# Score products of a stick-breaking attention: the second pass over 128 rows instead of 64

## Chip, cores and metric

One core of a Trainium2 chip runs the whole program. The metric is the device time of one execution in microseconds, as the median of the runs. Engine names: TensorE (PE; its weight loads are listed apart as PEld), VectorE (DVE), ScalarE (ACT), GpSimd (POOL) and SyncE (SP, which issues most DMAs).

## What is computed

One step of a two-layer hybrid network in float32, for 1024 prompt tokens and 8 sequences with 8 sample tokens each, width 1024. Layer 0 mixes by stick-breaking attention (16 heads of 64), layer 1 by an RWKV-7 recurrence; each is followed by a feed-forward block. The part that matters here is the prompt's attention of layer 0:

```python
z = (jnp.einsum('bqhd,bkhd->bhqk', q, k).astype(jnp.float32) * (SB_HEAD_DIM ** -0.5)
     + bias.astype(jnp.float32)[None, :, None, None])
mask = k_pos[None, :] < q_pos[:, None]
log_beta = jax.nn.log_sigmoid(z)
log_1mb = jnp.where(mask, log_beta - z, 0.0)
tail = lax.cumsum(log_1mb, axis=3, reverse=True) - log_1mb
a = jnp.where(mask, jnp.exp(log_beta + tail), 0.0)
return jnp.einsum('bhqk,bkhd->bqhd', a.astype(v.dtype), v)
```

So a weight is beta of its key times the product of 1 - beta over the later keys before the query.

## The kernel before

The tokens are worked on in two parts: the first has 576 prompt tokens, the second the other 448 and the 64 sample tokens. Features lie on the partitions, 128 to a feature tile; a feature tile holds two heads of 64.

Every dense layer (`dense`, L354 to L368) multiplies in three passes of rounded parts: a float32 value is split into an upper part (rounded to the fp32r format, "hi") and the lower rest ("lo"), and hi by hi, hi by lo and lo by hi are added up in one bank of PSUM (L364 to L366). After each such triple `step` is called; it advances a generator of background work by a number of yields. The prompt's attention is such background work: `background` (L1588) runs `attention(0)` at two yields a step and `attention(1)` at three, behind the projection of the second part and the output and feed-forward layers of the first. After `attention(1)` has done the prompt's queries, it goes on with the samples and the paged cache, in buffers that take the place of those of the prompt. The program is built with a framework that orders each engine's instructions by a simulated timeline (L1798) and puts in the semaphores; each engine then works through its own list in order.

For each of the eight feature tiles `att_stacks` (L526) loads q, k and v and prepares, for each of the two heads, with a the head's own 64 partitions and b the other 64:

- qh: the rounded upper part of q, on both halves (L546 on VectorE for a, L547 on ScalarE for b);
- kk: the upper part of k on a (L548) and its lower part on b (L549), both on VectorE;
- ql: the lower part of q on a (L550, GpSimd). One tile ql of 128 partitions serves both heads, half each.

q, k, qh, kk and ql have one buffer each, so the next feature tile's parts are written when the last products that read them are done.

`att_prompt` (L574) then goes over query tiles, the one of 64 queries first (both heads in one tile, q and k unsplit, L602), then those of 128 queries of one head. The keys are taken in pieces of up to 512. A score tile of one head is two passes into one bank of PSUM:

1. L604: qh by kk over 128 rows, which adds up hi(q) by hi(k) and hi(q) by lo(k);
2. L606: ql[a] by kk[a] over 64 rows, which adds lo(q) by hi(k).

`stick` (L555) follows: a sigmoid on ScalarE (L561) gives beta, the mask is laid on by GpSimd (L612 or L614), GpSimd makes 1 - beta (L564), with one column more at the end (L566 or L568), VectorE runs a multiplying scan from the last key to the first (L570) and multiplies beta by it (L571). TensorE transposes the weights (L127, called from L624), ScalarE copies them out of PSUM (L628), and TensorE multiplies them by v (L637). The output of a feature tile is copied to ot and written to DRAM (L642).

Of the kernel before, what the change touches and what calls it, by code (L numbers as in the profile page):

```python
# [10 lines left out]
F32 = mybir.dt.float32  # L11
# [9 lines left out]
NT = 8            # feature tiles of 128  # L21
TP = 1024         # prompt tokens
TS = 64           # sample tokens, column 1024 + 8 * sequence + step
T = TP + TS
PAGES = 16
ROWS = 2
# [19 lines left out]
class Part:  # L46
    """Columns o to o + W of the tokens, the first NP of them of the prompt; chunks of 64 tokens
    of the prompt from c0 on; ch: what fits into a bank of PSUM."""
# [45 lines left out]
class Kern:  # L94
# [19 lines left out]
    def copy(self, out, in_, eng=None):  # L114
        """PSUM or SBUF to SBUF, on ScalarE and VectorE in turn."""
        if eng is None:
            eng = "a" if self.flip() else "v"
        if eng == "a":
            self.nc.scalar.copy(out, in_)  # L119
        elif eng == "v":  # L120
            self.nc.vector.tensor_copy(out, in_)  # L121
        else:
            self.nc.gpsimd.tensor_copy(out, in_)
# [23 lines left out]
    def load_params(self, groups, tmp, ps, tag):  # L147
        """Vectors of features: rows of 128 on partitions, then features on partitions."""
# [46 lines left out]
    def behind(self, work, rate=1.0):  # L195
        """Work that goes on behind dense layers: rate steps of it behind every step of those."""
        self.work, self.rate, self.owed = work, rate, 0.0
# [11 lines left out]
    def beside(self, work, rate):  # L209
        """Other work beside dense layers, rate steps of it behind every step of those."""  # L210
        for _ in self.side:
            pass
        self.side, self.side_rate, self.side_owed = work, rate, 0.0

    def until(self, done):
        """The work behind, until done() (or its end)."""
        while not done():
            if next(self.work, self) is self:
                break
# [5 lines left out]
    def ada_steps(self, s, ps, tag, blocks=range(12)):  # L225
        """mod[:, j, v]: feature tile j of shift (0-7), scale (8-15), gate (16-23); vector v.
        The scale tiles end up as norm gain * (1 + scale)."""
# [44 lines left out]
    def rms(self, x, pt, tmp, ps, tag, slot, rslot=None):  # L272
        """1 / sqrt(mean square + eps) of every token, on all partitions: [128, W]."""
# [26 lines left out]
    def modulate(self, s, f, x, R, pt, t):  # L300
        """t = x * R * A of feature tile f, of samples with B added; returns B of the prompt."""
# [18 lines left out]
    def norm_split(self, s, x, R, pt, pool, tmp, slot):  # L320
        """Rounded parts of (x * R) * A + B."""
# [32 lines left out]
    def dense(self, w, mts, hi, lo, pt, ps, evac):  # L354
        """w: DRAM [K, M]; evac(m, c0, n, psum)."""
# [14 lines left out]
    def residual(self, s, x, pt, tmp):  # L370
        """evac of a dense layer: x += gate * out."""
# [17 lines left out]
    def load_x(self, pt, pool, ps, early):  # L389
        """Generator; the tiles are in self.x. early: all loads first."""  # L390
# [27 lines left out]
    def to_tokens(self, m, pt, t, dst_p, dst_s, tmp, ps):  # L418
        """Feature tile m of the columns of pt; rows of tokens to DRAM."""
# [43 lines left out]
    def load_split(self, src, pt, pool, tmp, parts):  # L463
        """Generator: rounded parts of feature tiles in DRAM."""
# [9 lines left out]
    def ahead(self, flag, src, pt, pool, tmp, xpool=None):  # L474
        """Generator: what the layer after a mixer needs, once the mixer is through: rounded parts
        of its output, and the tokens, to self.next."""
# [7 lines left out]
    def ffn(self, s, x, hi, lo, pt, pool, tmp, ps):  # L484
        """x += gate * (relu(h @ w_up) ** 2) @ w_down, the hidden layer 512 at a time."""
# [22 lines left out]
    def att_setup(self, lp):  # L508
# [7 lines left out]
        # of the two heads of a feature tile, 64 rows each  # L516
# [9 lines left out]
    def att_stacks(self, m, pt, sp):  # L526
        """Rounded parts of q and k of the two heads of tile m, the parts of k on top of each other."""
# [13 lines left out]
        ql = sp.tile([128, SLOT], F32R, tag="ql", name="ql")[:, :pt.NP]  # L541
        for hd in range(2):
# [6 lines left out]
            nc.vector.tensor_sub(kk[b], k[a], kk[a].bitcast(F32))  # L549
            nc.gpsimd.tensor_sub(ql[a], q[a], qh[a].bitcast(F32))  # L550
            qs.append(qh)
            ks.append(kk)
        return q, k, qs, ql, ks, v

    def stick(self, z, w, bias, bp, tag, carry, mask):  # L555
        """z: scores in PSUM [128, w], keys in order; returns weights a and the product of 1 - beta."""
# [17 lines left out]
    def att_prompt(self, m, pt, sp, bp, ps):  # L574
        """Generator over the query tiles (128 of a head, or 64 of both) of the two heads of tile m."""
        nc = self.nc
        q, k, qs, ql, ks, v = self.att_stacks(m, pt, sp)
# [7 lines left out]
        for c, end in sorted(tiles, key=lambda t: t[1] - t[0]):  # L585
# [7 lines left out]
            for j, (e0, e1) in enumerate(pieces):  # L593
# [3 lines left out]
                for x, hs in enumerate(heads):  # L597
                    z = ps.tile([128, 512], F32, tag="z", name="z")
                    for hd in hs:
                        a = self.R2[hd]  # L600
                        if both:
                            nc.tensor.matmul(z[a, :w], q[a, qc], k[a, e0:e1], start=True, stop=True)  # L602
                            continue
                        nc.tensor.matmul(z[:, :w], qs[hd][:, qc], ks[hd][:, e0:e1], start=True,  # L604
                                         stop=False)
                        nc.tensor.matmul(z[:, :w], ql[a, qc], ks[hd][a, e0:e1], start=False,  # L606
                                         stop=True)
# [44 lines left out]
    def page_k(self, sp, r):  # L652
        """[128 (feature / 256, key % 32), key / 32, feature % 256]"""
# [17 lines left out]
    def att_sample(self, sp, bp, ps):  # L671
        """Generator over the pieces (new keys, then two pages at a time, last pages first) of the
        sequences. Features are in 8 tiles of 128 rows (feature / 256, feature % 32), so that a
        page's blocks of 32 rows and columns, transposed by VectorE, are its transpose; tiles 2g and
        2g + 1 hold heads g, 4 + g, 8 + g and 12 + g. Rows of scores: g, head / 4, 8 queries; every g
        has its own columns of the tensor engine."""
# [12 lines left out]
        def queries(b):  # L689
            """Every head's queries in its own columns: [128, tile, 4 heads x 8]."""  # L690
# [56 lines left out]
        for n, (b, j) in enumerate(steps):  # L747
# [27 lines left out]
            if j == 0:  # L775
                # every row's own head, features on partitions
# [15 lines left out]
    def attention(self, i):  # L792
        """Generator: a half of the queries."""
# [72 lines left out]
    def rw_late(self, lp):  # L866
        """What the recurrence needs beyond rw_setup."""
# [11 lines left out]
    def xmix(self, n, f, h, e, pt, c0, w, t):  # L879
        """t = h + (previous token's h - h) * mu[n] of feature tile f, w columns of pt from c0;  # L880
        h starts e columns earlier."""
# [11 lines left out]
    def xsplit(self, n, pt, pool, tmp, parts):  # L893
        """Generator: rounded parts of the mixed input n, to parts."""
# [20 lines left out]
    def rw_norm(self, x, R, pt, pool, tmp):  # L915
        """The normalized input, to DRAM; rounded parts of the mixed input of r."""
# [34 lines left out]
    def rw_shift(self, tmp, ps):  # L951
        """The last token of every sequence."""
# [11 lines left out]
    def lora_mixed(self, ns, f, pt, c0, n, tmp):  # L964
        """Mixed inputs ns of feature tile f, n columns of pt from c0."""
# [10 lines left out]
    def lora_rates(self, pt, tmp, ps):  # L976
        """Generator: the narrow halves of the low-rank products of the rates."""
# [16 lines left out]
    def lora_gate(self, pt, pool, tmp, ps):  # L994
        """Generator: the narrow half of the low-rank product of the gate."""
# [23 lines left out]
    def rw_gate(self, pt, tmp, ps):  # L1019
        """Generator: the wide half of the gate, to DRAM."""  # L1020
# [16 lines left out]
    def dense_to(self, w, hi, lo, pt, tmp, ps, dst, then=None):  # L1037
        """Dense layer to DRAM, one feature tile at a time."""
# [9 lines left out]
    def rw_value(self, m, pt, t, tmp, ps):  # L1048
        """Feature tile m of v, tokens first."""
# [15 lines left out]
    def rw_keys(self, m, pt, k, pp, ps):  # L1065
        """Normalized keys of feature tile m."""
# [11 lines left out]
        # 1 / sqrt: from a guess by the exponent, three Newton steps  # L1078
# [20 lines left out]
    def rw_unit(self, m, i, pp, ps):  # L1099
        """Generator: the chunk products of feature tile m (two heads) that the state isn't needed  # L1100
        for. Rates are 1 + tanh of half the logits, twice the sigmoid."""
# [41 lines left out]
        # key  # L1143
# [9 lines left out]
        # decayed copies  # L1153
# [13 lines left out]
        # stacks: 0, 1 inputs of the solve, 2, 3 outputs, 4, 5 states; of the two heads  # L1167
# [52 lines left out]
    def rw_lanes(self, ms, pt, pool):  # L1220
        """Generator: (I - L)^-1 of diagonal blocks of 32 of the feature tiles ms, a block per
        partition (feature tile, block, head, chunk), by substitution."""
# [33 lines left out]
    def rw_units(self, i):  # L1256
        """Generator: chunk products of a half of the tokens."""
# [21 lines left out]
    def rw_chain(self, m, i, todo, cp, ps):  # L1279
        """Generator over the chunks of feature tile m: the recurrence of the state, and all that  # L1280
        follows up to w_o (put into todo)."""
# [24 lines left out]
        def inverse(n, st, tt, hv, L, x1):  # L1306
            """Inverses of 64 from those of 32."""
# [31 lines left out]
        for gi, (u, n) in enumerate(groups):  # L1339
# [4 lines left out]
            for cc in range(n):  # L1344
# [19 lines left out]
                # the state's rows still hold the chunk's first state  # L1364
# [46 lines left out]
    def rw_samples(self, m, y, cp, ps):  # L1411
        """Generator: the samples' chunk of feature tile m."""
# [11 lines left out]
        # the samples' states, key on partitions  # L1424
# [377 lines left out]
```

## Time and profile before

| what | value |
|---|---|
| median of 3 runs | 4046.95 us (4046.1 to 4064.11) |
| span of the profiled execution | 4045.0 us |
| span to median | 1.95 us |
| mean granted TensorE clock | 0.950 |
| L604, L606: number of each | 160 |
| time in which they run | 256 to 945 us |
| L550: number | 32 |

Profiled times count from the first instruction of the span. In the timeline a matmul's start and duration stand ahead of the engine; durations of matmuls that follow each other overlap, so the distance from start to start, called a step below, is what a matmul costs the engine in a row of them. `64*128 64x512` is a matmul of 64 rows and 128 columns of weights on 512 columns of moving data. A bracket at the end of a row gives the idle time before it and what ended it. In the list of waits the columns are the total in us, the number of times and the longest.

### The profile page before, as it was taken

The page shows a single profiled execution, that of the slowest core. Times are in us where ns is not written, and L with a number is a line of the kernel's source. Part 1 is how long each engine was busy: PE and PEld are TensorE (multiplying, and loading weights), DVE is VectorE, ACT ScalarE, POOL GpSimd, SP SyncE. Part 2 cuts the span into 40 slices and gives each one's busy share as a digit, 9 for nine tenths or more (in the row PEclk, how much of TensorE's full clock was granted, in tenths as well). Part 3 has the DMA queues.
Part 4 walks back from the last instruction along what each step waited for, and adds up shares of the span by engine and source line. Part 5 has one row for each costly group of instructions (what it writes and reads, how often), then busy time and mean ns, then how long its engine had stood idle before and what let it go on. Part 6 is the DMA issues. An engine that isn't in the chain of part 4 may idle for free. (4 is left out here: it accounts for less than half of the span.)

```text
span 4045.0 us, 76587 instructions
## 1 busy us (share of the span) xinstructions
PE 3675.1 (91%) x27756; PEld 2899.0 (72%) x27756; DVE 2499.4 (62%) x4907; ACT 1491.1 (37%) x3132; POOL 1322.8 (33%) x1844
## 2 busy tenths in 40 slices
PE   8989999899887888799779999999889999998998
PEld 6776667677666666577657777665688888876887
DVE  4256777886555455668775555677884666645444
ACT  4123444543121122455333444554434333433332
POOL 1135555563111111222243333433222222233442
PEclk9999999999999999799789999898899999999999
DMA  9965434125999999856645444556735444342332
GB/s 283 292 186 164 153 114 102 49 67 140 236 236 215 216 228 231 239 169 217 180 118 139 127 129 131 173 179 212 215 110 138 116 121 137 96 133 76 102 98 78
DMA packets 873728, 641.63 MB, mean 159 GB/s; under 512 B 174195, under 2 KB 793004, under 8 KB 873350
## 3 DMA queue, kind: packets, MB, share of 16 engines
q1 hardware_dynamic: 804198, 602.12, 52.8%
q10 hardware_dynamic: 69152, 34.61, 3.9%
q8 instruction: 220, 3.60, 0.4%
q14 instruction: 158, 1.29, 0.1%
HBM read 521.62 MB, written 114.92 MB: 157 GB/s over the span
## 5 line engine op out<-in xcount | busy, mean ns | idle before, releaser
L350 POOL TENSOR_TENSOR wl<-wst,wh 128x256 fp32r<-128x256 f32 (+1 forms) x512 | 641.3, 1254 | 1553.0 <-ACT wh L348 1353.0
L364 PE MATMUL dq<-hhi,wh 128*128 128x288 f32 (+1 forms) x2112 | 717.9, 341 | 29.4 <-ACT hhi L119 22.5
L348 ACT CAST wh<-wst 128x512 fp32r<-128x512 f32 (+1 forms) x512 | 424.6, 834 | 825.7 <-PE dq L365 546.2
L365 PE MATMUL dq<-hlo,wh 128*128 128x288 f32 (+1 forms) x2112 | 713.6, 338 | 7.7 <-POOL hlo L318 4.7
L366 PE MATMUL dq<-hhi,wl 128*128 128x288 f32 (+1 forms) x2112 | 715.9, 339 | 0.0
L365 PE MATMUL dq<-ul,wh 128*128 128x288 f32 (+1 forms) x1536 | 514.8, 335 | 0.0
L351 DVE TENSOR_TENSOR wl<-wst,wh 128x256 fp32r<-128x256 f32 (+1 forms) x512 | 349.5, 685 | 267.1 <-ACT wh L348 251.1
L366 PE MATMUL dq<-uh,wl 128*128 128x288 f32 (+1 forms) x1536 | 512.9, 335 | 0.0
L364 PE MATMUL dq<-uh,wh 128*128 128x288 f32 (+1 forms) x1536 | 511.2, 337 | 1.4 <-DVE x L379 0.6
L364 PEld LDWEIGHTS dq<-hhi,wh 128*128 128x128 f32 x2112 | 407.3, 193 | 72.9 <-ACT hhi L119 23.2
L365 PEld LDWEIGHTS dq<-hlo,wh 128*128 128x128 f32 x2112 | 406.9, 193 | 54.2 <-issue 14.4
L366 PEld LDWEIGHTS dq<-hhi,wl 128*128 128x128 f32 x2112 | 407.0, 193 | 49.5 <-issue 18.7
L379 DVE SCALAR_TENSOR_TENSOR x<-dq,mod,x 128x288 f32<-128x288 f32 (+1 forms) x432 | 243.2, 565 | 207.5 <-PE dq L366 204.8
L364 PEld LDWEIGHTS dq<-uh,wh 128*128 128x128 f32 x1536 | 292.2, 191 | 42.4 <-issue 14.1
L705 DVE STREAM_TRANSPOSE kT<-pagek 128x1024 f32<-128x1024 f32 x128 | 159.0, 1243 | 255.3 <-DMA pagek<-cache_k 240.5
L366 PEld LDWEIGHTS dq<-uh,wl 128*128 128x128 f32 x1536 | 293.1, 191 | 31.1 <-issue 8.3
L365 PEld LDWEIGHTS dq<-ul,wh 128*128 128x128 f32 x1536 | 292.7, 191 | 30.2 <-issue 8.5
L570 DVE TENSOR_TENSOR_SCAN prod<-prod 128x256 f32<-128x256 f32 (+5 forms) x264 | 259.6, 986 | 87.5 <-POOL prod L564 48.5
L564 POOL TENSOR_SCALAR prod<-beta 128x256 f32<-128x256 f32 (+5 forms) x264 | 169.2, 642 | 270.9 <-ACT beta L561 238.4
L364 PE MATMUL dq<-xhi,wh 128*128 128x288 f32 (+1 forms) x576 | 210.0, 365 | 4.5 <-DVE dn L121 2.1
L365 PE MATMUL dq<-xlo,wh 128*128 128x288 f32 (+1 forms) x576 | 203.4, 353 | 7.2 <-DVE xlo L318 5.5
L714 PE MATMUL zs<-kT,qbd 128*32 128x128 f32 x2048 | 95.4, 301 | 123.0 <-DVE kT L705 118.3
(327 smaller groups left out, 6684.4 us busy)
## 6 DMA issues: line engine op xcount, KB each, us to landing
pagek<-cache_k SPq DMA_DIRECT2D x512, 128.0 KB
pagev<-cache_v SPq DMA_DIRECT2D x128, 512.0 KB
wst<-w_up SPq DMA_DIRECT2D x96, 512.0 KB
wst<-w_down SPq DMA_DIRECT2D x192, 256.0 KB
st<-s_st SPq DMA_DIRECT2D x40, 672.0 KB
wst<-sb_w_qkv SPq DMA_DIRECT2D x48, 512.0 KB
adaw<-ada_w_mix SPq DMA_DIRECT2D x96, 256.0 KB
adaw<-ada_w_ffn SPq DMA_DIRECT2D x96, 256.0 KB
```

The costliest lines, as they stand in the source:

```text
L348: nc.scalar.copy(wh, st)
L350: nc.gpsimd.tensor_sub(wl[:, :h], st[:, :h], wh[:, :h].bitcast(F32))
L351: nc.vector.tensor_sub(wl[:, h:], st[:, h:], wh[:, h:].bitcast(F32))
L364: nc.tensor.matmul(q, wh[:, k, :], h, start=k == 0, stop=False)
L365: nc.tensor.matmul(q, wh[:, k, :], l, start=False, stop=False)
L366: nc.tensor.matmul(q, wl[:, k, :], h, start=False, stop=k == kt - 1)
L379: nc.vector.scalar_tensor_tensor(xs, q[:, :np_], g, xs, ALU.mult, ALU.add)
L564: nc.gpsimd.tensor_scalar(p[:, :w], beta[:, :w], -1.0, 1.0, ALU.mult, ALU.add)
L570: nc.vector.tensor_tensor_scan(r, r, r, 1.0 if carry is None else carry, ALU.mult, ALU.bypass)
L705: nc.vector.transpose(kT[-1].rearrange("p i m k -> p (i m k)"), t)
L714: nc.tensor.matmul(z[32 * g:32 * g + 32, 128 * pg:128 * pg + 128], qbd[:, m, :], kT[:, :, m, :], start=p == 0, stop=p == 1)
```

## The change

The lower part of q is made for each head on both halves of the partitions, in a buffer of its own per head, and the second pass multiplies all 128 rows of it by all 128 rows of kk. It thus adds lo(q) by lo(k), which was left out before. On GpSimd there are two subtractions per head instead of one. Nothing else in the program's source differs but comments.

```diff
@@ att_stacks
         qs, ks = [], []
-        ql = sp.tile([128, SLOT], F32R, tag="ql", name="ql")[:, :pt.NP]
         for hd in range(2):
             a, b = self.R2[hd], self.R2[1 - hd]
             qh = sp.tile([128, SLOT], F32R, tag=f"qh{hd}", name="qh")[:, :pt.NP]
...
             nc.vector.tensor_sub(kk[b], k[a], kk[a].bitcast(F32))
+            ql = sp.tile([128, SLOT], F32R, tag=f"ql{hd}", name="ql")[:, :pt.NP]
             nc.gpsimd.tensor_sub(ql[a], q[a], qh[a].bitcast(F32))
-            qs.append(qh)
+            nc.gpsimd.tensor_sub(ql[b], q[a], qh[a].bitcast(F32))
+            qs.append((qh, ql))
             ks.append(kk)
-        return q, k, qs, ql, ks, v
+        return q, k, qs, ks, v
@@ att_prompt
-        q, k, qs, ql, ks, v = self.att_stacks(m, pt, sp)
+        q, k, qs, ks, v = self.att_stacks(m, pt, sp)
...
-                        nc.tensor.matmul(z[:, :w], qs[hd][:, qc], ks[hd][:, e0:e1], start=True,
-                                         stop=False)
-                        nc.tensor.matmul(z[:, :w], ql[a, qc], ks[hd][a, e0:e1], start=False,
-                                         stop=True)
+                        for i, part in enumerate(qs[hd]):
+                            nc.tensor.matmul(z[:, :w], part[:, qc], ks[hd][:, e0:e1], start=i == 0,
+                                             stop=i == 1)
```

## The prediction

> **What bounds the kernel now.** I read the page first (span, share of each engine), then where the two changed lines run, then the engines in that stretch, the waits there, and last the timeline of TensorE around a few score products.
>
> ```profile
> span 4045.0 us, 76587 instructions
> ```
>
> and, from its first part:
>
> ```profile
> PE 3675.1 (91%) x27756; PEld 2899.0 (72%) x27756; DVE 2499.4 (62%) x4907; ACT 1491.1 (37%) x3132; POOL 1322.8 (33%) x1844
> ```
> The span is 4045.0 us; the runs' median, 4046.95, is 1.95 us above it. TensorE is busy for 91%. Where the changed products stand (duration min/median/max in ns, first and last start in us):
>
> ```profile
> L604 PE MATMUL z<-kk,qh x160: 224/418/667, 256.1 to 944.8; 128*128 128x512 f32 x80, 128*128 128x256 f32 x32, 128*128 128x384 f32 x32, 128*128 128x128 f32 x16
> L606 PE MATMUL z<-kk,ql x160: 322/490/792, 256.4 to 945.2; 64*128 64x512 f32 x80, 64*128 64x256 f32 x32, 64*128 64x384 f32 x32, 64*128 64x128 f32 x16
> L550 POOL TENSOR_TENSOR ql<-q,qh x32: 1123/1500/2912, 67.6 to 902.8; 64x576 fp32r<-64x576 f32 x16, 64x448 fp32r<-64x448 f32 x16
> ```
> There are 160 pairs of passes, all between 256 and 945 us, and 32 subtractions that make ql. The second pass (64 rows) has a median of 490 ns against 418 of the first (128 rows). The engines in that stretch, split where the second half's tiles begin, and two slices at its end (us busy of PE, PEld, DVE, ACT, POOL; clock; DMA share; GB/s):
>
> ```profile
> 247.00:600.00 353.00, 331.15 (x2065) 234.42 (x2065) 242.70 (x350) 140.46 (x290) 184.26 (x333) 0.96 0.46 138
> 600.00:948.00 348.00, 325.74 (x2349) 247.73 (x2350) 298.12 (x376) 166.02 (x313) 198.34 (x296) 0.97 0.26 74
> 940.00:960.00 20.00, 20.00 (x156) 16.38 (x156) 11.30 (x16) 7.28 (x16) 4.17 (x7) 1.00 0.05 14
> 960.00:980.00 20.00, 19.31 (x168) 18.27 (x166) 9.86 (x20) 4.21 (x7) 8.68 (x23) 1.00 0.95 227
> ```
> TensorE is busy for 94% of both halves and idle for 22 us in each. VectorE is at 69% in the first half (242.70 of 353) and at 86% in the second (298.12 of 348): it is the next bound there. The last two rows say what comes behind: the DMA load jumps from 0.05 to 0.95 only when the prompt's attention ends and its buffers go to the pages, so what is saved before 948 us moves the rest forward and is not eaten by a transfer that already runs. The waits in 247 to 948 us (total us, times, longest):
>
> ```profile
> PEld z L606 <- issue: 27.6, 116, 0.5
> PE tq L127 <- DVE beta L571: 14.4, 12, 2.5
> ```
> The weight load of the 64-row pass stands idle 116 times for nothing but its turn; TensorE itself waits little for VectorE's weights beta (14.4 us).
>
> **The change: what it removes on TensorE.** Starts of one engine's matmuls, in us (then the duration):
>
> ```profile
> 509.78 0.39 PE L366 MATMUL dq<-hhi,wl 128*128 128x512 f32 x1
> 510.01 0.39 PE L364 MATMUL dq<-hhi,wh 128*128 128x512 f32 x1
> 510.25 0.40 PE L604 MATMUL z<-kk,qh 128*128 128x512 f32 x1
> 510.57 0.49 PE L606 MATMUL z<-kk,ql 64*128 64x512 f32 x1
> 510.99 0.50 PE L365 MATMUL dq<-hlo,wh 128*128 128x512 f32 x1
> 511.33 0.40 PE L366 MATMUL dq<-hhi,wl 128*128 128x512 f32 x1
> 511.57 0.40 PE L364 MATMUL dq<-hhi,wh 128*128 128x512 f32 x1
> ```
> Full-height matmuls of 512 columns follow each other at 0.235 us (509.78 to 510.25 in two steps). Around the 64-row pass the steps are 0.32, 0.42 and 0.34, then 0.24 again. From 510.25 to 511.57 four matmuls take 1.32 us where four at 0.235 would take 0.94: a pair costs 0.38 us more than it would with no change of height. The changed second pass has the shape of the first, so I take all 0.38 as removed. The Trainium skill ("TensorE: Matmul & The Clock Gate", section "Why this matters for your kernels") says the opposite: a matmul with 32 rows takes the same time as one with 128. By that the second pass would become no cheaper, and the edit would bring only its cost on GpSimd; the rows above do not agree, since 0.42 stands against 0.235 at the same 512 columns.
>
> For 256 columns:
>
> ```profile
> 503.15 0.36 PE L604 MATMUL z<-kk,qh 128*128 128x256 f32 x1
> 503.44 0.38 PE L606 MATMUL z<-kk,ql 64*128 64x256 f32 x1
> 503.75 0.38 PE L604 MATMUL z<-kk,qh 128*128 128x256 f32 x1
> 504.07 0.38 PE L606 MATMUL z<-kk,ql 64*128 64x256 f32 x1
> 504.38 0.50 PE L366 MATMUL dq<-hhi,wl 128*128 128x512 f32 x1
> ```
>
> For 384 columns:
>
> ```profile
> 506.34 0.42 PE L604 MATMUL z<-kk,qh 128*128 128x384 f32 x1
> 506.69 0.44 PE L606 MATMUL z<-kk,ql 64*128 64x384 f32 x1
> 507.06 0.55 PE L127 MATMUL tokq<-cst,dn 128*128 128x128 f32 x3
> ```
>
> And dense matmuls of 288 columns:
>
> ```profile
> 651.06 0.29 PE L366 MATMUL dq<-shi,wl 128*128 128x288 f32 x1
> 651.18 0.29 PE L364 MATMUL dq<-shi,wh 128*128 128x288 f32 x1
> 651.32 0.29 PE L365 MATMUL dq<-slo,wh 128*128 128x288 f32 x1
> ```
> Two pairs of 256 columns take 1.23 us (503.15 to 504.38). No row shows 256 columns at full height undisturbed; the nearest, 288 columns, step at 0.13, so four would take 0.52: 0.36 saved a pair. A pair of 384 takes 0.72; between 0.13 and 0.235 I take 0.18 a step: 0.36 saved. For the 16 pairs of 128 columns I take 0.3, an estimate below these. Sum: 80 x 0.38 + 64 x 0.36 + 16 x 0.3 = 58 us.
>
> Not all of it goes where a matmul of another shape follows:
>
> ```profile
> 501.30 0.39 PE L365 MATMUL dq<-hlo,wh 128*128 128x512 f32 x1
> 501.61 1.09 PE L637 MATMUL o<-aT,v 128*64 128x128 f32 x14
> ```
> Ahead of the products with v, of 64 columns, a step is 0.31 and not 0.235 whatever stood before. If one pair in eight keeps half of its 0.38, an estimate from the mixed order in these rows, 4 us stay. **Gross: 54 us**, 21 in the first half (16 pairs each of 128, 256, 384 and 512 columns: 22) and 33 in the second (16 of 256, 16 of 384, 64 of 512: 36).
>
> **What it adds.** Per feature tile two more subtractions on GpSimd (ql on the other half of the partitions), 32 in all, in the shape of L550. In this stretch:
>
> ```profile
> L550 POOL TENSOR_TENSOR ql<-q,qh 64x448 fp32r<-64x448 f32 (+1 forms) x30 | 49.0, 1633 | 16.4 <-PE z L606 13.6 <-DVE qh L546 1.3 <-issue 0.4
> ```
> At 1633 ns each that is 52 us of GpSimd, 26 a half: 184 becomes 210 of 353, 198 becomes 224 of 348, no bound by its total. What is queued behind the two new instructions (3.3 us a tile) is seen where a tile starts:
>
> ```profile
> 715.14 2.13 POOL L550 TENSOR_TENSOR ql<-q,qh 64x448 fp32r<-64x448 f32 x1
> 717.37 1.41 POOL L564 TENSOR_SCALAR prod<-beta 128x512 f32<-128x512 f32 x1
> ```
>
> and on TensorE:
>
> ```profile
> 724.81 0.66 PE L127 MATMUL tq<-cst,beta 128*128 128x128 f32 x4 [0.80 <-DVE beta L571]
> ```
> The chain beta, 1 - beta (L564), scan (L570), product (L571) stands behind ql on GpSimd, and TensorE's transposes (L127) end it; here they came 0.80 us late already. Ends for the 16 tiles: nothing, if dense matmuls that stand before the transposes cover it (TensorE is 94% busy), and 16 x 3.3 = 52 us, if none is covered; a gain is no end, since work is only added. I take a quarter, 13 us, nearer to nothing, because with 30 such subtractions in place the transposes wait for beta only 12 times in all.
>
> The new instructions also run against VectorE:
>
> ```profile
> 444.84 3.31 POOL L550 TENSOR_TENSOR ql<-q,qh 64x576 fp32r<-64x576 f32 x2 [3.80 <-PE z L606]
> 444.85 2.00 DVE L549 TENSOR_TENSOR kk<-k,kk 64x576 fp32r<-64x576 f32 x1
> ```
>
> and the next one:
>
> ```profile
> 448.71 0.74 DVE L549 TENSOR_TENSOR kk<-k,kk 64x576 fp32r<-64x576 f32 x1
> ```
> The same subtraction on VectorE took 2.00 us beside ql and 0.74 away from it: it seems to stand still while GpSimd's subtraction runs. The Trainium skill ("SBUF — State Buffer", section "Who interferes with whom") has this as a rule: a VectorE instruction with two inputs in SBUF and a GpSimd instruction that reads SBUF share one port, and the second blocks fully. The row agrees: 1.26 us lost beside a ql of some 1.65.
>
> So of 26 us in the second half VectorE loses between 0 and 26; I take 13: 298 + 13 = 311 us of VectorE. If its share can't rise above today's 86%, the half lasts 363 us, 15 longer; at 100% it would last 311, and TensorE's own 33 would be had in full. In the middle, at 93.5%, it lasts 333: 15 us saved, with the tile starts of that half in it. In the first half VectorE is no bound: 21 less half of the 13, 15 us.
>
> The rest: ql gets a buffer per head, so the first head's subtraction waits for that head's passes alone; the 13.6 us of that wait are GpSimd's and bring TensorE nothing by themselves. No DMA, no ScalarE work and no wait is added. The program's order on each engine is made anew by the scheduler; that can't be priced by a row, except that the idle time that it could add to or take from is the 22 us in each half. **Net: 15 + 15 = 30 us.** 4045.0 - 30 = 4015 for the span, and 4017 with the 1.95 us between span and median.
>
> **Rivals.** All by the same 4047.
> 1. Everything is had: dense work covers GpSimd, VectorE packs tighter. For it: TensorE waits for beta only 14.4 us. Against it: 86% VectorE. 4047 - 54 = 3993.
> 2. VectorE and GpSimd take the place of TensorE in both halves: the second half gains nothing, the first keeps half of its 15. For it: 298 of 348. 4047 - 8 = 4039, no change that counts.
> 3. Slower: at each tile start the two new subtractions are paid twice in series, once as GpSimd's delay of the chain (52 us) and once as VectorE's standstill inside it (52 us). 104 - 54 = 50: 4097. It decides from 54/16 = 3.4 us lost per tile, and is plainly slower from (54 + 20)/16 = 4.6. For it: 444.84 to 448.71, where both happen. Against it: TensorE goes on there with dense matmuls.
> 4. The change doesn't do what it says: the steps around the second pass stay at 0.32 to 0.42 because they belong to switching from dense to score products and not to the height. Then only the cost is left, 0 to 13: 4047 to 4060. Against it: the step into the first pass, 510.01 to 510.25, is an ordinary 0.24. The rule of the Trainium skill named above ("TensorE: Matmul & The Clock Gate", on matmuls of few rows) comes to this rival's time.
>
> **How the numbers follow.** The measurement tells about 0.5% (20 us) from no change: faster is below 4027, slower above 4067. Forecast (10 to 45 us gained) 0.47, of which a tenth is gained by less than 20; rival 1 0.16, rival 2 0.24, rival 3 0.08, rival 4 0.05. Faster: 0.42 + 0.16 = 0.58 and a little of rival 2's spread, 0.60; same 0.32; slower 0.08. The range goes from 3990, below the full gain, to 4050, over rival 2 and the lower part of rival 4; rival 3, the rest of rival 4 and a gain above 57 are left out, some 0.15. The likeliest case's own range is 4002 to 4037.
>
> **What would show it.** In the profile after, the second pass is 128*128 and steps of 0.24 follow each other through both passes, with the PEld wait on issue (27.6) gone; POOL has 64 subtractions of about 1.6 us, together near 105 us; the last score product lies near 915 us instead of 945; VectorE's share from 600 us on is above 90%; the wait of the transposes for beta is above 14.4 us but not above 40. I am wrong if the steps stay above 0.3 (rival 4), if the steps are short and the last score product is still near 940 (rival 2), or if the waits for beta grow past 50 us (rival 3).

## The result, and the profile after

The kernel after takes 4086.51 us (median of 4 runs, 4080.07 to 4092.01) against 4049.95 us for the kernel before beside it: a ratio of 1.0088, 95% interval 1.0067 to 1.0109. It is slower by 0.9%; the forecast of 4017 us and its range to 4050 were wrong, and in the wrong direction.

The page of the kernel after, span and first part:

```profile
span 4082.8 us, 76578 instructions
PE 3655.5 (90%) x27756; PEld 2914.0 (71%) x27756; DVE 2514.5 (62%) x4907; ACT 1481.5 (36%) x3130; POOL 1392.7 (34%) x1876
```

TensorE is busy for 19.6 us less than before (3655.5 against 3675.1), and the span is 37.8 us longer: its idle time rose from 370 to 427 us. So the edit did take work off TensorE, and on this page the loss stands as idle time. The second passes, in the view of their line (duration min/median/max in ns, first and last start):

```profile
L607 PE MATMUL z<-kk,ql x160: 273/387/562, 259.2 to 956.8; 128*128 128x512 f32 x80, 128*128 128x256 f32 x32, 128*128 128x384 f32 x32, 128*128 128x128 f32 x16
```

and of the added subtractions:

```profile
L552 POOL TENSOR_TENSOR ql<-q,qh x32: 1145/1820/2017, 71.9 to 919.0; 64x576 fp32r<-64x576 f32 x16, 64x448 fp32r<-64x448 f32 x16
```

The second pass has 128 rows now and a median of 387 ns instead of 490, but the last score product starts at 956.8 us, not at the forecast 915 and not even at the 945 of before. The timeline of TensorE around a pair of 256 columns shows that the steps did what they should:

```profile
509.75 0.36 PE L607 MATMUL z<-kk,qh 128*128 128x256 f32 x1
509.95 0.28 PE L607 MATMUL z<-kk,ql 128*128 128x256 f32 x1
510.06 0.28 PE L607 MATMUL z<-kk,qh 128*128 128x256 f32 x1
510.18 0.28 PE L607 MATMUL z<-kk,ql 128*128 128x256 f32 x1
510.30 0.38 PE L127 MATMUL tokq<-cst,dn 128*128 128x128 f32 x2
```

After a first step of 0.20 they are 0.11 to 0.12 us, where before they were 0.29 to 0.32. The engines by stretch (columns as before: PE, PEld, DVE, ACT, POOL busy, clock, DMA share, GB/s):

```profile
247.00:957.00 710.00, 632.31 (x4517) 501.86 (x4516) 559.48 (x733) 305.01 (x609) 452.94 (x660) 0.95 0.36 106
...
600.00:948.00 348.00, 306.71 (x2390) 258.29 (x2389) 307.99 (x381) 162.81 (x315) 237.51 (x308) 0.96 0.27 74
```

and the waits of the transposes:

```profile
PE tq L127 <- DVE beta L573: 32.6, 24, 2.9
PEld tq L127 <- DVE beta L573: 28.6, 19, 3.0
```

In the second half TensorE is idle for 41 us instead of 22, and the transposes wait 32.6 us for beta instead of 14.4. The weight load's wait "on issue" at the second pass, 27.6 us before, is almost gone; in after one line stands for both passes:

```profile
PEld z L607 <- issue: 3.8, 20, 0.4
```

Note the counts in brackets: 4517 matmuls ran in this stretch, and 4412 ran from 247 to 948 before. The stretch holds more dense work than before (1820 of these matmuls write the tile dq of the dense layers, against 1710), so part of its length is only another order of the work. That makes the end of the attention a poor measure, and the experiments had to separate order and work.

### The profile page after: what moved, and what is told of

Same layout as the page of the kernel before. It is cut to its first block, busy times and chain, and to the rows that moved or that the text cites. A ratio compares the mean times of both kernels' runs of the same rounds, so it can differ in the third digit from the quotient of the medians.

```text
span 4082.8 us, 76578 instructions
## 1 busy us (share of the span) xinstructions
PE 3655.5 (90%) x27756; PEld 2914.0 (71%) x27756; DVE 2514.5 (62%) x4907; ACT 1481.5 (36%) x3130; POOL 1392.7 (34%) x1876
## 4 chain that ended last, share of the span: by engine, by line
PE 47%; DMA 15%; DVE 9%; issue 4%; SPq 3%; ACT 2%; POOL 1%; DVEq 0%; ACTq 0%; POOLq 0%
PE dq L364 12%; PE dq L365 12%; PE dq L366 12%; DMA pagek<-cache_k 6%; DMA wst<-w_down 2%; DMA wst<-w_up 1%; DMA pagev<-cache_v 1%; DVE kT L706 1%; SPq L658 1%; PE tq L127 1%; PE qc L1364 1%; DVE wl L351 1%; DVE lxn L1246 1%; DVE tm L1244 1%; PE qc L1354 1%
## 5 line engine op out<-in xcount | busy, mean ns | idle before, releaser
L366 PEld LDWEIGHTS dq<-uh,wl 128*128 128x128 f32 x1536 | 294.4, 192 | 32.6 <-issue 9.4
L572 DVE TENSOR_TENSOR_SCAN prod<-prod 128x256 f32<-128x256 f32 (+5 forms) x264 | 260.5, 991 | 86.0 <-POOL prod L568 42.8
L566 POOL TENSOR_SCALAR prod<-beta 128x256 f32<-128x256 f32 (+5 forms) x264 | 179.7, 682 | 240.1 <-ACT beta L563 224.8
L500 ACT CAST uh<-ut 128x288 fp32r<-128x288 f32 (+1 forms) x192 | 95.0, 495 | 308.5 <-DVE ut L498 300.1
```

Source lines behind the costliest of these rows:

```text
L366: nc.tensor.matmul(q, wl[:, k, :], h, start=False, stop=k == kt - 1)
L500: nc.scalar.copy(a, t[:, :n])
L566: nc.gpsimd.tensor_scalar(p[:, :w], beta[:, :w], -1.0, 1.0, ALU.mult, ALU.add)
L572: nc.vector.tensor_tensor_scan(r, r, r, 1.0 if carry is None else carry, ALU.mult, ALU.bypass)
```

## The experiments

The theories were these. **One**: the instructions cost what they cost, and the scheduler's new order (the step of the prediction that had no price) carries the loss; the expectations call this theory A. **Two**: the second subtraction on GpSimd costs more than the 24 us allowed for it, through the chain of beta or through VectorE. **Three**: the 128-row pass brings little. Theory two is theory B of the expectations; their other letters are explained where they stand. All three could hold in part, so the first need was to fix the order.

Between successive instructions of every engine, order-only edges were added, which no engine waits for at run time and which the scheduler must keep; the order itself comes from building the other kernel first. New instructions stand right behind the subtraction that was there before. The kernel before was run again beside each group of runs, so its median varies a little (4048.62 to 4052.32 us); the ratios compare runs of one group.

```diff
+for p, i in zip(seq, seq[1:]):
+    tc.add_manual_dep(i, p.name, mybir.DependencyInfo(
+        mybir.DependencyClass.NoSync, mybir.DependencyReason.DATA), reason="order")
```

**The change in the order of before.** The instructions of after, every engine's order from before.

> The changed kernel, its instructions issued on every engine in the order of the kernel before (order-only edges; the new subtraction stands right behind the old one). Theory A (the scheduler's new order costs the time; the change itself, in a given order, saves up to the 54 us of TensorE less what GpSimd adds): 4005 to 4050 us, the last score product before 945 us. Theory B (the new subtractions cost more on GpSimd and VectorE than TensorE saves, whatever the order): 4080 to 4095 us, the waits of the transposes for beta far above 14 us.

Measured: 4054.31 us against 4052.32, ratio 1.0002 (0.9988 to 1.0016). With the order held, the change does nothing that can be measured.

**Before in the order of after.** No instruction is changed, only their order.

> The kernel before (64-row second pass, one subtraction), its instructions issued on every engine in the order of the changed kernel. Theory A: 4080 to 4120 us, since it has the order that costs and not the saving on TensorE. Theory B: 4040 to 4055 us, as the kernel before.

Measured: 4088.51 against 4052.32, 1.0095 (1.0074 to 1.0117). The page of this kernel:

```profile
span 4081.6 us, 76531 instructions
PE 3690.8 (90%) x27756; PEld 2908.0 (71%) x27756; DVE 2489.4 (61%) x4907; ACT 1486.2 (36%) x3130; POOL 1327.3 (33%) x1844
```

The kernel before becomes as slow as the kernel after by order alone: some 36 us with the same instructions. The whole loss of the result lies there. TensorE is busy for 15.7 us more than before in this order (3690.8 against 3675.1) and idle for 20.9 us more. Against this kernel the one after has 35.3 us less of busy time (3655.5), so the 19.6 us above understate what the edit took off TensorE.

**The 128-row pass alone.** The other half of ql holds zeros, written once in each part's attention, in a buffer for each head; the second pass has 128 rows and computes what it computed before (lo(q) by hi(k), plus zero). No second subtraction.

```diff
+self.ql0 = [sp.tile([128, SLOT], F32R, name=f"qlz{hd}") for hd in range(2)]
...
+ql = self.ql0[hd][:, :pt.NP]
 nc.gpsimd.tensor_sub(ql[a], q[a], qh[a].bitcast(F32))
+if m == 0:
+    nc.gpsimd.memset(self.ql0[hd][b].bitcast(F32), 0.0)
...
-nc.tensor.matmul(z[:, :w], ql[a, qc], ks[hd][a, e0:e1], start=False, stop=True)
+nc.tensor.matmul(z[:, :w], ql[:, qc], ks[hd][:, e0:e1], start=False, stop=True)
```

> TensorE's part alone in the order of the kernel before: the second pass over 128 rows, the other half of ql zero from the start of each half's attention on (four memsets in all), no second subtraction, a ql for each head. Theory A: 4000 to 4030 us; the prompt's attention ends 20 to 45 us earlier and the pages start as much earlier. Theory B: the same 4000 to 4030 us, since the cost is left out. Theory C (the saving goes to dense layers that must then wait for the pages, which the DMA queues bound): 4040 to 4055 us.

Measured: 4022.02 against 4052.32, 0.9931 (0.9907 to 0.9955), 30 us faster. No run has the buffer per head alone in the order of before, so what it brings is inside these 30 us. The stretch from 247 us to the last beta of the prompt's attention, first in before and then in this kernel; since the order is the same, both hold the same work:

```profile
247.00:948.00 701.00, 656.90 (x4412) 482.15 (x4413) 540.81 (x725) 306.48 (x603) 382.60 (x628) 0.97 0.36 106
```

```profile
247.00:922.00 675.00, 611.45 (x4404) 481.56 (x4404) 538.62 (x723) 302.29 (x602) 398.87 (x630) 0.95 0.38 110
```

and the waits that grew, first in before (its wait for beta is 14.4 us) and then in this kernel:

```profile
PE o L637 <- DMA v<-v_prompt: 2.8, 2, 2.5
PE o L637 <- DVE ot L121: 1.8, 2, 1.0
```

```profile
PE tq L131 <- DVE beta L587: 23.7, 20, 3.0
PE o L655 <- DMA v<-v_prompt: 7.2, 4, 5.1
PE o L655 <- DVE ot L125: 5.8, 5, 1.8
```

TensorE's busy time fell by 45.5 us (656.90 to 611.45), but its idle time rose by 19.5 (44.1 to 63.6): the attention ended 26 us earlier. Nearly half of what TensorE saved turned into waits although nothing but two fills of 0.57 us had been added in this stretch to the other engines. The transposes wait 9.3 us longer for beta, and the products with v 4.4 us longer for the load of v and 4.0 us longer for the copy of their last output. The page transposes, first in before and then in this kernel:

```profile
L705 DVE STREAM_TRANSPOSE kT<-pagek x128: 1186/1245/1248, 974.5 to 1689.1; 128x1024 f32<-128x1024 f32 x128
```

```profile
L723 DVE STREAM_TRANSPOSE kT<-pagek x128: 1187/1245/1248, 948.9 to 1667.1; 128x1024 f32<-128x1024 f32 x128
```

The first came at 948.9 instead of 974.5 us and the last at 1667.1 instead of 1689.1, so most of the saving passed through the page stage, where the DMA share is 0.95. In this traced execution the lead at the end is 15 us (spans of 4029.8 and 4045.0); it took 4031.51 us, 9.5 more than its kernel's median, so what single traces say of the rest of the program is good to some 10 us.

**The same in an order of its own.**

> The same without a given order: the scheduler makes its own. Theory A: anywhere from 4000 to 4095 us, by the order that comes out, and not the time of the run in the order of the kernel before. Theory B: 4000 to 4030 us, near that run.

Measured: 4028.98, 0.9942 (0.9919 to 0.9965). This order is also a new one, made for a program with four instructions more (the fills), and in sum it costs little or nothing. The sum has two parts that cancel, as the table at the joined orders shows.

**The second subtraction alone, in the order of before.** A buffer per head and the new subtraction, whose result nobody reads; the second pass stays at 64 rows.

```diff
 nc.gpsimd.tensor_sub(ql[a], q[a], qh[a].bitcast(F32))
+nc.gpsimd.tensor_sub(ql[b], q[a], qh[a].bitcast(F32))
```

> GpSimd's part alone in the order of the kernel before: the second pass stays at 64 rows, but ql is made on both halves for each head (the other half is read by nobody). Theory A2 (in a given order the change is the sum of two parts, TensorE's gain of 30 us and a like cost of the subtractions): 4075 to 4090 us. Theory D (the subtractions alone are hidden behind TensorE and cost only once TensorE is faster): 4050 to 4060 us.

Measured: 4084.42 against 4048.62, 1.0078 (1.0061 to 1.0095): 36 us. The added group, VectorE's subtraction for kk in the groups of this kernel (x count, busy us, mean ns, idle):

```profile
L570 POOL TENSOR_TENSOR ql<-q,qh 64x448 fp32r<-64x448 f32 (+1 forms) x30 | 52.0, 1733 | 2.0
...
L556 DVE TENSOR_TENSOR kk<-k,kk 64x1024 fp32r<-64x1024 f32 (+1 forms) x30 | 46.1, 1538 | 0.9
```

and the stretch to its last beta:

```profile
247.00:982.00 735.00, 666.82 (x4421) 489.47 (x4421) 566.18 (x725) 307.18 (x602) 430.92 (x658) 0.95 0.35 101
```

52 us more of GpSimd's queue make the attention 34 us longer. VectorE is busy for 25 us more in it (540.81 to 566.18) with the same instructions; its subtraction for kk took 1538 ns in the mean and 1286 before, 7.5 of these 25 us. The shift stays much as it is from there to the end: 34 us at the end of the attention, 35 at the last page transpose (1724.1 against 1689.1), 40 at the end of the traced execution, 36 in the medians and 32 by the ratio. With the 128-row pass as the base, the subtraction costs the same: 4054.31 less 4022.02 is 32 us. The two parts add up, and in the order of before they cancel (30 saved, 32 to 36 paid).

**GpSimd time without reading.** Zero half, order of before, and per tile and head two fills of 64x576 with zeros in place of the subtraction.

```diff
+for _ in range(2):
+    nc.gpsimd.memset(self.ql0[hd][b].bitcast(F32), 0.0)
```

> As zero_half_in_order_of_before, but with two memsets of the other half of ql per head and tile on GpSimd, right behind the subtraction (about 0.6 us each, so 1.2 to 1.4 us, near the 1.1 to 1.2 us that a subtraction takes undisturbed); they read no SBUF. Theory P (the subtractions cost because VectorE's two-input instructions stand still while GpSimd reads SBUF): 4020 to 4030 us, as with the zero half alone. Theory G (they cost as time in GpSimd's queue, ahead of 1 - beta and the masks): 4040 to 4055 us.

Measured: 4032.56 against 4048.62, 0.9956 (0.9937 to 0.9975).

**GpSimd time with reading.** The same with copies of the half of zeros onto itself.

```diff
+for _ in range(2):
+    nc.gpsimd.tensor_copy(ql[b], ql[b].bitcast(F32))
```

> As fills_in_order_of_before, but the two memsets per head and tile are two copies on GpSimd of the zeros onto themselves, so that GpSimd reads SBUF as the subtraction does. Theory P (most of the subtractions' cost comes from VectorE standing still while GpSimd reads): 4040 to 4055 us, and VectorE's subtraction for kk as long as beside the doubled ql (1.5 us and not 1.35). Theory G (GpSimd's time alone): as the run with memsets if the copies take as long, 4025 to 4038 us.

Measured: 4056.19 against 4049.16, 1.0011 (0.9998 to 1.0025). The groups of both, first the fills:

```profile
L566 POOL MEMSET qlz<- 64x576 f32 x60 | 38.3, 639 | 3.4
...
L556 DVE TENSOR_TENSOR kk<-k,kk 64x1024 fp32r<-64x1024 f32 (+1 forms) x30 | 40.5, 1352 | 0.9
```

and the copies:

```profile
L567 POOL CAST qlz<-qlz 64x448 fp32r<-64x448 f32 (+1 forms) x60 | 58.1, 968 | 3.7
...
L557 DVE TENSOR_TENSOR kk<-k,kk 64x1024 fp32r<-64x1024 f32 (+1 forms) x30 | 43.8, 1459 | 0.9
```

The costs below are differences of ratios to the zero half's (0.9931), in us, with bounds from the two intervals (the root of the sum of their squares). VectorE's busy time is that from 247 us to the last beta, with 723 or 724 instructions each:

| added on GpSimd | GpSimd us | cost us | cost per GpSimd us | mean of VectorE's kk subtraction, ns | VectorE busy, us |
|---|---|---|---|---|---|
| nothing | 0 | 0 | | 1282 | 538.6 |
| fills | 38.3 | 10 (-2 to 22) | 0.27 | 1352 | 541.0 |
| copies | 58.1 | 32 (21 to 44) | 0.55 | 1459 | 554.7 |
| subtractions | 52 | 29 (18 to 40); by medians 32 | 0.55 to 0.61 | 1530 | 565.5 |

The copies cost 22 us more than the fills (13 to 32, by the bounds of both). VectorE's time grows by 2.4 us beside fills, by 16 beside copies and by 27 beside subtractions: that reading on GpSimd lengthens VectorE's work, and writing alone hardly does, is shown. The price of writing alone is not: its 10 us come with bounds that include zero. It would be a quarter of the fills' time, the share that the prediction took for the tile starts. The fills are also 20 us shorter than the copies, so how much of the copies' cost is queue and how much is reading is not settled.

**The buffer per head alone, in an order of its own.**

> The kernel before with one thing changed, a ql buffer for each head; 64-row pass, one subtraction, the scheduler's own order. The work on the engines is that of the kernel before. Theory A (the order is a lottery of some 40 us, drawn anew by any edit): more than 10 us away from the kernel before, either way, between 4010 and 4095 us. Theory E (only the added subtractions and their modelled time lead to the bad order): 4042 to 4062 us.

Measured: 4055.26 against 4048.62, 1.0015 (1.0000 to 1.0031). Its order is the zero half's own but for the latter's four memsets, and it departs from that of before from about 400 to 3600 us. In sum this reordering costs, at most, 0.3%.

**The second subtraction in an order of its own.**

> The 64-row pass with the second subtraction and a ql for each head, in the scheduler's own order. Theory E (the added subtractions lead the scheduler to the order that costs): 4105 to 4130 us (4084 in the given order, and some 36 more). Theory A (each edit draws another order): 4060 to 4100 us.

Measured: 4112.81 against 4049.16, 1.0145 (1.0126 to 1.0163). Each engine has the order of the kernel after; the only difference is the height of the second pass. The time is the one that theory E of the expectations gives, and the order itself follows from the added subtractions: the two kernels with them got one order, and the two without them (zero half and buffers) got another. Whether the loss follows from the subtractions too is another question, which the table at the joined orders answers. The pass is worth 4112.81 less 4086.51, 26 us (23 by the ratios), in this order too.

**Where in the program the order costs.** The kernel before, in its own order for the first 53% of the instructions (to about 2100 us, behind the pages and into layer 1), then in the order of after.

> The kernel before, in its own order for the first 53% of the instructions, then in the order of the changed kernel. Theory F (the order of the changed kernel costs in the recurrence of layer 1, which the change does not touch): 4070 to 4090 us. Theory H (it costs in the attention, and what is later is only the debt from there): 4045 to 4060 us.

Measured: 4087.5 against 4049.16, 1.0078 (1.0060 to 1.0096): nearly the whole cost, from a part of the program that the change does not touch. Windows of before, then of this kernel:

```profile
1750.00:2150.00 400.00, 323.86 (x2161) 263.21 (x2160) 296.57 (x629) 164.92 (x324) 129.00 (x126) 0.88 0.59 171
2150.00:2750.00 600.00, 589.12 (x4316) 432.24 (x4315) 363.28 (x891) 290.37 (x679) 222.34 (x305) 0.98 0.52 151
2750.00:3150.00 400.00, 359.92 (x2630) 297.85 (x2631) 286.35 (x665) 160.26 (x340) 105.52 (x120) 0.91 0.57 164
```

```profile
1750.00:2150.00 400.00, 328.41 (x2151) 264.39 (x2151) 298.31 (x631) 165.19 (x323) 128.51 (x125) 0.86 0.58 167
2150.00:2750.00 600.00, 579.62 (x4217) 420.88 (x4215) 349.22 (x854) 273.24 (x655) 217.65 (x300) 0.96 0.51 147
2750.00:3150.00 400.00, 350.73 (x2463) 288.76 (x2463) 281.89 (x648) 160.41 (x321) 100.03 (x113) 0.90 0.58 166
```

To 2150 us the two do the same amount of matmuls (2161 and 2151); in the next 1000 us the second falls behind by 266 matmuls and TensorE is idle for 19 us more. The groups of TensorE from 2150 to 2310 us, before:

```profile
L366 PE MATMUL dq<-hhi,wl 128*128 128x512 f32 x85 | 33.9, 399 | 0.0
...
L1372 PE MATMUL qc<-hv,st 128*64 128x64 f32 x76 | 6.7, 244 | 0.0
```

and in this kernel:

```profile
L372 PE MATMUL dq<-hhi,wl 128*128 128x512 f32 x64 | 25.7, 402 | 0.7 <-POOL wl L356 0.7
...
L1402 PE MATMUL qc<-hv,st 128*64 128x64 f32 x88 | 8.3, 266 | 0.5 <-DVE hv L127 0.5
```

In 160 us one dense layer got through 64 instead of 85 matmuls of this pass; more of the recurrence's products stand between them (88 instead of 76 of this line), each with a longer mean (266 against 244 ns). TensorE's busy time grows with it over the whole span, 3694.8 us for the 27756 matmuls that took 3675.1, as the page of this kernel says:

```profile
PE 3694.8 (90%) x27756; PEld 2912.0 (71%) x27756; DVE 2505.9 (61%) x4907; ACT 1486.5 (36%) x3130; POOL 1318.8 (32%) x1844
```

The granted clock of these two traced executions, 0.950 and 0.941, may have a part in the longer durations; the loss itself is hardly the clock's, since the traced execution of before in the order of after had 0.945, within the 0.940 to 0.951 of the runs of before, and took 4083.38 us. What in that order is at fault beyond this is open; no run changed it piece by piece.

**Two joined orders.** If the order of layer 1 matters and is independent of what comes ahead, the zero half's own order to 53% and the order of before behind it should be best. First with the zero half, then with the instructions of after.

> The zero half of the runs before, issued in its own order for the first 53% of the instructions (about the first 2100 us, by which that run was 56 us ahead of the kernel before and from which on it fell back to 22), then in the order of the kernel before. Theory A (what was lost from there on is the order's): 3985 to 4005 us. If the lead at 2100 us was only dense work done early, owed by the background: 4015 to 4035 us.

> The changed kernel with all its parts, in the order of zero_half_joined_order (which took 4004 us with the zero half). If order and parts add up: 4004 + 31 for the subtractions = 4025 to 4045 us, faster than the kernel before with the very change that made it slower. If the parts depend on the order: anywhere from 4010 to 4080 us.

Measured: 4003.74 against 4048.62, 0.9884 (0.9866 to 0.9901), the fastest version of the study, 45 us below before; and 4039.6 against 4049.16, 0.9974 (0.9959 to 0.9989). The kernel after is thus a little faster than before in a better order, and the second subtraction takes 36 us of what the 128-row pass gives there too. The attention of the first of them, and its waits for beta:

```profile
247.00:918.00 671.00, 611.38 (x4455) 487.86 (x4454) 540.65 (x729) 303.71 (x606) 403.14 (x631) 0.96 0.38 111
```

```profile
PE tq L132 <- DVE beta L592: 14.2, 16, 1.7
```

In this order the transposes wait 14.2 us for beta and not 23.7: how much of TensorE's saving gets through depends on the order too.

The traces also say what the two new orders have in common. The table has how far each traced execution lies behind before (a minus sign: ahead of it) when ScalarE casts weight tile 179, which before does at 2036.0 us, and at the end of the span:

| instructions | order | at weight tile 179, us | at the end, us | lost in between, us |
|---|---|---|---|---|
| zero half | of before | -16.4 | -15.2 | 1.2 |
| second subtraction, 64 rows | of before | 39.2 | 40.0 | 0.8 |
| zero half | own, then of before | -45.4 | -43.0 | 2.4 |
| after | own order of zero half, then of before | -10.2 | -8.0 | 2.2 |
| before | of after | 1.2 | 36.6 | 35.4 |
| after | own | 1.6 | 37.8 | 36.2 |
| second subtraction, 64 rows | own | 17.6 | 68.1 | 50.5 |
| before | of before, then of after | 11.5 | 42.8 | 31.3 |
| buffers | own | -26.1 | 3.5 | 29.6 |
| zero half | own | -48.1 | -21.7 | 26.4 |

Both orders that the scheduler made anew lose 26 to 51 us behind this point, the one without the second subtraction too (26 and 30); the order of before loses 0.8 to 2.4 us against itself with other instructions, and in the three traces that the table leaves out (after, copies and fills in the order of before) 3.9, -6.4 and 3.9. What sets the two apart is in part the size of this loss and in part what comes ahead of it: the order of buffers and zero half had gained 26 us (buffers) and 32 us (zero half against zero half in the order of before) and so comes out near even; the order of after had gained nothing with the instructions of before, 14 us with those of after and 22 us with the second subtraction alone, and does not. So a loss in layer 1 isn't a mark of the added subtractions. The order of before is the best of the three there, and no run says why.

## Why the prediction was wrong

The forecast was 30 us faster; the result is 37 us slower. The runs split these 67 us into four terms, of which three lie in the steps that had a price and one in the step that had none.

**The gross saving of TensorE, 54 us: right in kind, a little high.** Step and shape were as forecast, the wait of the weight load fell from 27.6 to 3.8 us, and the busy time of TensorE in the stretch fell by 45.5 us in a fixed order (8.5 less); with the second subtraction in both kernels, by 45.2 (666.82 to 621.58). Rival 4, that nothing would be saved, is refuted, and with it the rule of the Trainium skill ("TensorE: Matmul & The Clock Gate", section "Why this matters for your kernels") as a forecast for this case: the pass with 128 rows alone, against 64, is 0.7% faster.

**Dense work as cover for the shorter scores: failed.** The prediction let TensorE's saving in the first half through in full and charged only the additions. The zero half adds next to nothing, and 19.5 of its 45.5 us still went into idle time: TensorE reaches its transposes and its products with v earlier, and beta, v and the output's copy do not come as much earlier. VectorE's share had been priced as a bound of the half as a whole, 86% to 100%, but in the kernel after it is 88.5% in the second half (307.99 of 348), below the 90% that was to show. It never became the bound by its total; the chain by tile was late.

**The additions, 24 us (13 for tile starts, some 11 for VectorE): too low.** They cost 32 to 36 us by the medians and 29 to 36 by the ratios: 36 (32) without the 128-row pass, 32 (29) with it, and 36 in the joined order. The prediction's 52 us of GpSimd is what ran (52.0 us), and its interference with VectorE was shown: 25 us of VectorE in the whole stretch (540.81 to 566.18), where the prediction took 13 in the second half and VectorE for no bound in the first. The fills put some 10 us on the queue alone, near the 13 of the tile starts but with bounds from -2 to 22. So the part that was too small is most likely the one that goes with reading SBUF. The rule of the Trainium skill named in the prediction ("SBUF — State Buffer", section "Who interferes with whom") stands behind it: the table above agrees with it, since VectorE's two-input subtraction lengthens by 177 to 248 ns beside copies and subtractions. It lengthens by 70 ns beside fills too, which the rule does not give, and no run says why.

With the additions at 32, these three make 8.5 + 19.5 + 8 = 36 us, and turn the 30 us gained at the end of the attention into 6 lost: 954.1 us for the kernel after in the order of before, against 947.8. The 45.5 and 19.5 are of single traces and the 32 is of medians, so this sum is good to some 10 us; the medians have no change that can be measured there (1.0002).

**The order, "can't be priced by a row, except that the idle time that it could add to or take from is the 22 us in each half": failed, and it decides the sign.** It costs 36 us, or 32 by the difference of 4086.51 and 4054.31; with these the four terms come to 68 to 72 us, where 67 were to be explained. The bound was false for its place: the scheduler makes the order of the whole program anew, and the loss against before arises behind 2036 us, in layer 1, where the change has no instruction. The bound looked at the stretch of the change alone. Chance has a part in the sign: the order of before is better in layer 1 than both others that the scheduler made, so the edit had little to win from a new order there, and only a gain ahead of it, as in the order of buffers and zero half, could make up for the loss.

**"What is saved before 948 us moves the rest forward": right in a given order** (26 us at the end of the attention, 22 at the last page transpose, 15 at the end of the trace, 28 to 30 in ratio and medians). In the scheduler's own order it is not, because the work after it is no longer the same. The kernel after shows this in the page stage. Windows of before and after:

```profile
1600.00:1700.00 100.00, 74.70 (x733) 54.23 (x737) 69.14 (x105) 39.71 (x66) 26.40 (x39) 0.78 0.96 259
```

```profile
1600.00:1700.00 100.00, 59.43 (x633) 38.91 (x632) 65.25 (x93) 37.54 (x64) 24.74 (x36) 0.78 0.95 254
```

Its dense layers had been up to 22 us ahead (the cast of weight tile 72 at 900.0 instead of 921.9 us), as the 105 matmuls more in the attention say; its pages were not, with the first transpose at 984.9 instead of 974.5 us. Here, where DMA is busy for 95% of the time in both, TensorE stands idle for 15 us more, and the lead is gone by 1750 us (the cast of weight tile 160 at 1749.1 against 1751.3). In this trace a lead of the dense layers in front of a stage that the transfers bound was worth nothing.

**The rivals.** Rival 3 came to 4097 and the sign that happened, but by another mechanism: a standstill paid twice would have made the change slow in the order of before, and there it is 1.0002. Rival 2, no change that counts (4039), describes the change in a fixed order best, for a reason near its own. No rival had the scheduler in it. Of the signs that the prediction named, the short steps and a wait for beta between 14.4 and 40 us (32.6) came; neither could show a loss in layer 1. Two readings in its working are slightly off without a part in the miss: the stretch to 600 us holds 73 of the pairs and not 64, and halfway between 86% and 100% is 93%, which makes 14 us and not 15.

## What to carry to other kernels

An edit in a program whose order a scheduler makes has two effects, that of its instructions and that of the new order, and the second can lie anywhere behind the edit and be as large as the first. A new order that costs nothing in sum can still hold a gain and a loss, and joining two orders shows them: 4003.74 us against 4028.98 and 4022.02 with either order alone. Hold the order with order-only edges to measure the instructions, and try the instructions before in the new order to measure the order. A saving on the busiest engine is worth what the chain beside it lets through: here 26 of 45 us in the order of before. The 128 rows are better had with a half of zeros written once than with a second subtraction for every tile.

## What the hardware showed

- A matmul of 64 rows among those of 128 rows costs more than a full one: at 512 columns the steps around it were 0.32, 0.42 and 0.34 us against 0.235. With zeros in the other 64 rows the same result took 45.5 us less of TensorE over 160 passes, 0.28 us a pass. No run separates the height itself from the change of height between neighbours.
- GpSimd work that reads SBUF lengthens VectorE's work beside it: in the stretch of the attention 58.1 us of copies added 16 us and 52 us of subtractions 27 us to VectorE's busy time, 38.3 us of fills 2.4 us. Each us of copies or subtractions cost the kernel 0.55 to 0.61 us; the cost of the fills is within the noise.
- The same 27756 matmuls had a busy time of 3675.1, 3690.8 or 3694.8 us in three orders, at granted clocks of 0.950, 0.945 and 0.941.
